# Two layers of mixing and experts: where the modulation blocks, entry loads and sums' zeroing are placed

## The chip, the cores and the metric

One core of one Trainium2 chip. The metric is the time of one execution of the whole kernel on the device, in microseconds (us); less is better. Engines are named as in the profile: PE (TensorE), PEld (its weight loads), DVE (VectorE), ACT (ScalarE), POOL (GpSimd) and SP (the queue that issues most DMAs).

## The reference

Two blocks of different kinds run one after the other on 512 tokens of width 1024, in float32. The change concerns the first, which has two layers and carries 256 context tokens beside the 512.

```python
sc, scc = silu(c), silu(c_ctx)[None]
for i in range(2):
    mods  = sc  @ ada_w[i] + ada_b[i]      # 1024 -> 6 x 1024: sh1, sc1, g1, sh2, sc2, g2
    cmods = scc @ ada_w[i] + ada_b[i]
    h  = rms_norm(x, n1) * (1 + sc1) + sh1            # the same for the context
    p  = h @ w_in                                     # 11 pieces: a_b a_c a_h b_v b_g c_q c_k c_v d_q d_k d_v
    y  = [short conv of a, gated conv of 31 taps of b, window attention of c, global attention of d]
    x  = x + g1 * (y @ w_out)
    h2 = rms_norm(x, n2) * (1 + sc2) + sh2
    x  = x + g2 * expert_choice_ffn(h2)               # 16 experts, each takes its top tokens
```

In the expert step each of 16 experts chooses 64 of the 512 tokens (and, in the first layer, 32 of the 256 context tokens) by a softmax over a router, computes silu(h w_gate) * (h w_up) w_down for them and adds the weighted rows back. Only the first layer updates the context. The modulation vectors are made in 12 blocks of 512 columns each per layer: blocks 0 and 1 are sh1, 2 and 3 sc1, 4 and 5 g1, 6 and 7 sh2, 8 and 9 sc2, 10 and 11 g2.

## The kernel before

All of it is one program; the framework gives every engine its own list of instructions, in an order that it lays out from the order of the Python statements, and puts in the waits. An engine runs its list strictly in order. SP's list holds nearly all loads, so a load whose buffer is not free holds back the loads behind it.

**Modulation blocks.** `ada_gen` (L309) does one block per two steps. A block needs four loads of 512 KB (`ada_load`, L191), 16 PE instructions at L318 (four side by side in column groups), a copy on ACT (L323), four transposes (L327) and two small DVE operations (L329, L330) that leave the vectors in `M[l]`. Loads go into tiles of the pool `wp`, which has five buffers of 512 KB named `raw`; dense weights and five of the expert weight slots use the same five. `ada_gen` also loads the next block ahead (L320).

**Entry (L236 to L398).** SP issues small row loads (gains, biases, conv weights, gathered in `rows` and transposed to columns in `cols` by `rows_to_cols`, L347) mixed with the loads of x, then the four blocks 0, 2, 1 and 3 of layer 0 into a tile of their own, `ada0`, with the context and the first dense weights between them. The key weights of attention c come in one load. The query weights come in two loads of 64 columns (pieces of 256 bytes) per unit. Five row loads are issued by POOL. Each of the six token tiles is scaled by its root mean square and transposed. When all four blocks are done, `norm1_first` (L386) makes the 8 k-slices of the normed input as a high part `hh0` (ACT) and a low part `hl0` (DVE for x, POOL for the context).

**Dense products.** `dense` (L421) goes through units of 128 output columns. Each unit's weights are loaded (`load`), split in two halves into a high part `wh` (ACT, L442) and a low part `wl` (POOL, L443), and multiplied in three products per k-slice (L473, and L475 for the context). `ahead` sets how far in front of the unit the loads run: with 4, one unit ahead after the first four; with None, three.

**Mixing (`layer`, L602).** 18 units of the input projection (order c_k, c_q, c_q, c_v, b, d, a) run interleaved, step by step by fixed shares (`run_all`, L943 to L947), with the attention (`att_gen`), the 31-tap convolution on DVE (`conv31`) and, in layer 0 only, the modulation blocks 4 to 11 of layer 0 and 0 to 7 of layer 1. Layer 0 passes `ahead=4`, layer 1 None. Before it, xT and xcT are stored to DRAM (L621) so that their place can be used, and POOL loads a table (L638) that the rotary step waits for. The output projection (8 units, L999) follows and fills in the expert weights' first loads.

**Routing and experts (`experts`, L1022).** Expert weights come as units of 512 KB, 24 per expert, through a ring of 18 `rawA`, five `raw` and two `rawB` buffers in layer 0 (20, 5 and 8 in layer 1), one new load for each unit that PE has used (`wload`, L1042). In layer 0, 18 are loaded at the start; the five raw ones follow at L1182, as the raw buffers first serve blocks 8 to 11 of layer 1, which are done in steps inside the routing: after the affinities (L1120) and between top-k rounds (L1150). Normed rows are written to `hd` in DRAM, two sum tensors in DRAM are zeroed (3 MB, L1134 to L1139), DVE finds the top tokens, and POOL gathers the rows (L1209), which PE transposes (L1221). Then per expert: gate units, down units of the expert before, up units. In layer 0 the outputs are added into the sums in DRAM by POOL's queue. Near the end the sums are loaded back (`sums_load`, L1305; two buffers) and added to x and the context in 12 halves (`sums_add`, L1310): the four context halves in the up units of expert 15, the eight of x in its down units.

Of the kernel before, what the change touches and what calls it, by code (L numbers as in the profile page):

```python
# [10 lines left out]
F32 = mybir.dt.float32  # L11
# [123 lines left out]
def main_kernel(ctx, tc, I, out, stop=None, dbg=None, manual=False):  # L135
# [37 lines left out]
    dx = pool(ctx, "dx", space=DRAM).tile([128, 8 * 768], F32)  # L173
# [47 lines left out]
    ada0 = ent.tile([128, 4, 4, 1024], F32)  # L221
# [20 lines left out]
    x_load(1)  # L242
    row_load(G, 0, "qn", I["q_norm_g"], 2, dup=True)
    row_load(G, 0, "kn", I["k_norm_g"], 2, dup=True)
    row_load(G, 0, "cbb", I["conv_b_b"].rearrange("l (h p) -> (l h) p", p=128), 4)
    row_load(G, 0, "lng", I["conv_ln_g"].rearrange("l (h p) -> (l h) p", p=128), 4)
    row_load(G, 0, "lnb", I["conv_ln_b"].rearrange("l (h p) -> (l h) p", p=128), 4)
# [3 lines left out]
    x_load(2)  # L251
    SY.dma_start(sinkb, bass.AP(tensor=I["sink"].tensor, offset=I["sink"].offset, ap=[[0, 128], [1, 8]]))
    row_load(SY, 0, "fg", I["final_g"].rearrange("(k p) -> k p", p=128), 8)
    row_load(SY, 0, "ln1", I["ln1_2"].rearrange("l (k p) -> (l k) p", p=128), 8)
    x_load(3)
# [3 lines left out]
    ada_load(0, 0, ada0[:, 0], hfs=(0, 1))  # L259
    row_load(SY, 3, "cq", I["conv_qkv_2"].rearrange("l t (h p) -> (l t h) p", p=128), 48)  # L260
    row_load(SY, 3, "fc", I["ffn_conv_2"].rearrange("l t (h p) -> (l t h) p", p=128), 66)
    ada_load(0, 0, ada0[:, 0], hfs=(2, 3))
    ada_load(0, 2, ada0[:, 2])
    for t in range(2):
        SY.dma_start(cin[:, t, :], I["ctx"][0, t * 128:(t + 1) * 128, :])
    ada_load(0, 1, ada0[:, 1])
    pre0 = {}
    pre0[0] = raw_tile().rearrange("p (k c) -> p k c", k=8)
    SY.dma_start(pre0[0], I["w_in"][0, :, 1536:1664].rearrange("(k p) c -> p k c", p=128))
    pre0[1] = raw_tile().rearrange("p (k c) -> p k c", k=8)  # L270
    for h in range(2):
        SY.dma_start(pre0[1][:, :, 64 * h:64 * h + 64],
                     I["w_in"][0, :, 1280 + 128 * h:1344 + 128 * h].rearrange("(k p) c -> p k c", p=128))
    ada_load(0, 3, ada0[:, 3])
# [34 lines left out]
    def ada_gen(l, blocks, pl, psp):  # L309
        g, o, n = RO["adab"]  # L310
        for b in blocks:
# [8 lines left out]
            if 3 < b < 11 or (l == 1 and b != 7 and b < 11):  # L320
                ada_load(l, b + 1, hfs=range(4 if l == 1 and b > 7 else 3))
# [10 lines left out]
            yield  # L332

# [7 lines left out]
    if True:  # L341
        with ExitStack() as e0:
# [4 lines left out]
            def rows_to_cols(g, n):  # L347
                p = pse.tile([128, 512], F32, name="rc")
                T.transpose(p[:, :n], rows[0:n, g, :], ident[0:n, 0:n])
                V.tensor_copy(cols[:, g, 0:n], p[:, :n])  # L350

            rows_to_cols(0, 16)
            A.activation(s2[:, :, 0], col("c"), AF.Silu)
            A.activation(s2[:, :, 1], col("cc"), AF.Silu)
            ga = ada_gen(0, (0, 2, 1, 3), sqp, pse)
            ss = ent.tile([128, 6], F32)
            for t in range(6):
# [16 lines left out]
                if t == 1:  # L374
                    rows_to_cols(1, RO["n", 1])
# [4 lines left out]
            for g in (0, 2, 3):  # L380
                rows_to_cols(g, RO["n", g])
            V.tensor_scalar(nsink, sinkb, -1.0, None, op0=OP.mult)

        entry.close()

        def norm1_first(sqp):  # L386
            a1 = sqp.tile([128, 8, 2], F32, name="a1")
            for k in range(8):
# [32 lines left out]
        def dense(units, hh, hl, dw, dps, la=3, pre={}, ahead=None):  # L421
# [5 lines left out]
            def load(i):  # L427
                if i in pre:
                    raw[i] = pre[i]
                elif i < len(units):  # L430
                    raw[i] = raw_tile().rearrange("p (k c) -> p k c", k=8)
                    units[i][0](raw[i])

            def split(i):
                if i < len(units):
                    nk = units[i][4] if len(units[i]) > 3 else 8
                    hi[i] = []
                    for a in range(0, nk, 4):
# [3 lines left out]
                        A.activation(wh[:, :n], raw[i][:, a:a + n], AF.Copy)  # L442
                        G.tensor_tensor(wl[:, :n], raw[i][:, a:a + n], wh[:, :n].bitcast(F32), op=OP.subtract)  # L443
# [41 lines left out]
        def colload(src, c0, n=128):  # L485
            def f(raw):
                SY.dma_start(raw[:, :, 0:n], src[:, c0:c0 + n].rearrange("(k p) c -> p k c", p=128))
            return f

        def colload2(src, ca, cb):  # L490
            def f(raw):
                for h, c in enumerate((ca, cb)):
# [529 lines left out]
        def experts(l, rwpA, lg, rbias, a2, nA, nB):  # L1022
# [37 lines left out]
            if has:  # L1060
                ada_load(1, 8)
# [908 lines left out]
```

## Time and profile before

| | us |
|---|---|
| three runs | 2655.12, 2669.66, 2670.03 |
| median | 2669.66 |
| profiled execution, own time | 2663.15 |
| its span, first to last instruction | 2660.6 |

The span is divided like this (from windows and timelines): entry to 48, first mixing and its output projection to 457, routing to 501, first experts to 1075, second mixing and projection to 1360, second routing and experts to about 1890, then the second block. A busy time is what the profile counts for an engine; matmuls overlap, so PE can be "busy" without being at its peak. In a timeline row, the bracket holds the engine's idle time before the instruction and what ended it.

### The profile page before, as it was taken

How to read it: one execution, taken by the hardware profiler on the slowest of the kernel's cores; microseconds unless marked ns; L12 is line 12 of the kernel's file. 1: busy time of each engine (PE TensorE's matmuls, PEld its weight loads, DVE VectorE, ACT ScalarE, POOL GpSimd, SP SyncE). 2: the span in 40 equal slices, each digit the busy share in tenths (PEclk: the TensorE clock that was granted, in tenths of full speed). 3: DMA queues.
4: the chain of work that ended last, by engine and by line, in shares of the span. 5: the costliest groups of instructions: out<-in, count | busy, mean ns of one | idle time of the engine just before them, and what ended most of it. 6: DMA issues, size and time to landing. Idle time of an engine off the chain costs nothing.

```text
span 2660.6 us, 41308 instructions
## 1 busy us (share of the span) xinstructions
PE 2472.6 (93%) x16415; PEld 1498.3 (56%) x16415; DVE 1091.2 (41%) x2371; ACT 870.0 (33%) x1769; POOL 637.3 (24%) x552
## 2 busy tenths in 40 slices
PE   6999999799999999799979989898899999999998
PEld 3776777344444333677743212132578787888876
DVE  4488853311111114689641201021674555444411
ACT  4534362211111111465532111110552435434322
POOL 3423112011111100633220000000433323444443
PEclk9999999899999999799989999999899999999999
DMA  8455455999999998221279999999321102333321
GB/s 284 136 163 141 148 191 195 320 385 387 387 386 385 388 389 296 61 60 48 84 285 391 394 400 400 399 404 408 108 64 27 38 25 72 95 95 96 98 84 63
DMA packets 324758, 584.08 MB, mean 220 GB/s; under 512 B 36864, under 2 KB 190007, under 8 KB 323927
## 3 DMA queue, kind: packets, MB, share of 16 engines
q1 hardware_dynamic: 311943, 555.16, 57.6%
q0 software_dynamic: 12480, 26.23, 4.1%
q8 instruction: 129, 2.11, 0.3%
q14 instruction: 62, 0.51, 0.1%
q10 hardware_dynamic: 144, 0.08, 0.0%
HBM read 556.74 MB, written 18.87 MB: 216 GB/s over the span
## 4 chain that ended last, share of the span: by engine, by line
PE 65%; DMA 18%; DVE 9%; issue 3%; POOL 2%; ACT 1%; SPq 1%; ACTq 0%; DVEq 0%; POOLq 0%
PE px L473 20%; PE ax L1243 4%; DMA rawA<-in_w_down_dram 4%; PE yx L1243 3%; PE ux L1243 3%; PE g L473 2%; DMA rawA<-in_w_up_dram 2%; PE y L584 2%; PE px L475 2%; DMA rawA<-in_w_gate_dram 2%; PE s L553 2%; PE ux L1237 2%; PE pt L565 2%; PE ac L1248 2%; PE ax L1237 2%
## 5 line engine op out<-in xcount | busy, mean ns | idle before, releaser
L443 POOL TENSOR_TENSOR wl<-raw,wh 128x512 fp32r<-128x512 f32 (+1 forms) x312 | 408.7, 1313 | 968.0 <-ACT wh L442 908.2
L442 ACT ACTIVATE wh<-raw 128x512 fp32r<-128x512 f32 (+1 forms) x312 | 193.7, 625 | 440.5 <-PE px L473 207.7
L473 PE MATMUL px<-hh,wh 128*128 128x512 f32 x768 | 314.2, 410 | 6.4 <-DVE xT L1401 1.8
L473 PE MATMUL px<-hh,wl 128*128 128x512 f32 x768 | 311.8, 406 | 6.5 <-POOL wl L443 6.5
L473 PE MATMUL px<-hl,wh 128*128 128x512 f32 x768 | 313.7, 409 | 4.1 <-DVE hl L1019 1.9
L1225 ACT ACTIVATE xt<-tr,mod,a 128x64 f32<-128x64 f32 x256 | 87.0, 405 | 297.6 <-PE tr L1221 287.3
L473 PEld LDWEIGHTS px<-hh,wh 128*128 128x128 f32 x768 | 147.8, 193 | 40.9 <-issue 6.1
L473 PEld LDWEIGHTS px<-hh,wl 128*128 128x128 f32 x768 | 147.9, 193 | 39.5 <-POOL wl L443 7.2
L473 PEld LDWEIGHTS px<-hl,wh 128*128 128x128 f32 x768 | 148.2, 193 | 37.8 <-issue 3.8
L1369 DVE SCALAR_TENSOR_TENSOR Yx<-yx,gcol,Yx 64x512 fp32r<-64x512 f32 x36 | 27.0, 750 | 266.9 <-ACT Yx L1368 266.9
L1209 POOL DMA_INDIRECT xg<-hd,gidx x32 | 29.7, 928 | 432.2 <-PE tr L1221 399.0
L785 DVE SCALAR_TENSOR_TENSOR yT<-ub,cols,yT 128x512 f32<-128x512 f32 (+1 forms) x180 | 126.3, 717 | 0.6
L1243 PE MATMUL ax<-rawA,xt 128*32 128x512 f32 x856 | 117.2, 596 | 1.9 <-DMA rawA<-in_w_gate_dram 1.9
L1273 ACT ACTIVATE sa<-ax 128x512 f32<-128x512 f32 x32 | 19.1, 597 | 287.8 <-PE ax L1243 182.7
L1300 POOL DMA_INDIRECT sumx<-ys,place x14 | 22.0, 1571 | 376.7 <-ACT ys L1347 376.7
L1243 PE MATMUL ux<-rawA,xt 128*32 128x512 f32 x800 | 106.1, 594 | 0.9 <-DMA rawA<-in_w_up_dram 0.9
L1237 PE MATMUL ux<-rawA,xt 128*64 128x512 f32 x328 | 87.5, 611 | 8.3 <-DMA rawA<-in_w_up_dram 8.2
L1237 PE MATMUL yx<-rawA,hT 128*64 128x512 f32 x316 | 80.7, 610 | 12.6 <-DMA rawA<-in_w_down_dram 11.8
L565 PE MATMUL pt<-tab,P 128*128 128x128 f32 x448 | 83.7, 288 | 7.0 <-DVE PT L571 4.3
L1368 ACT ACTIVATE Yx<-yx,gcol 64x512 fp32r<-64x512 f32 x36 | 24.6, 682 | 191.1 <-PE yx L1237 139.3
L1228 DVE TENSOR_SCALAR xt<-tr,a,mod 128x32 f32<-128x32 f32 x128 | 39.1, 310 | 114.7 <-ACT xt L1225 114.2
L1237 PE MATMUL ax<-rawA,xt 128*64 128x512 f32 x316 | 77.4, 612 | 8.1 <-DMA rawA<-in_w_gate_dram 7.5
(593 smaller groups left out, 4887.5 us busy)
## 6 DMA issues: line engine op xcount, KB each, us to landing
rawA<-in_w_gate_dram SPq DMA_DIRECT2D x186, 512.0 KB
rawA<-in_w_up_dram SPq DMA_DIRECT2D x182, 512.0 KB
rawA<-in_w_down_dram SPq DMA_DIRECT2D x151, 512.0 KB
raw<-in_ada_w_dram SPq DMA_DIRECT2D x80, 512.0 KB
raw<-in_w_down_dram SPq DMA_DIRECT2D x74, 512.0 KB
raw<-in_w_gate_dram SPq DMA_DIRECT2D x62, 512.0 KB
raw<-in_w_in_dram SPq DMA_DIRECT2D x56, 512.0 KB
raw<-in_w_up_dram SPq DMA_DIRECT2D x55, 512.0 KB
```

The costliest lines, as they stand in the source:

```text
L442: A.activation(wh[:, :n], raw[i][:, a:a + n], AF.Copy)
L443: G.tensor_tensor(wl[:, :n], raw[i][:, a:a + n], wh[:, :n].bitcast(F32), op=OP.subtract)
L473: T.matmul(px, lhsT=w[:, k % 4, :], rhs=h[:, k0 + k, 0:512], start=st, stop=sp_)
L475: T.matmul(pc, lhsT=w[:, k % 4, :], rhs=h[:, k0 + k, 512:nt], start=st, stop=sp_)
L553: T.matmul(s[:, :w], lhsT=q, rhs=k, start=(a == 0), stop=(a == len(mm) - 1))
L565: T.transpose(pt[:, (t - a) * 128:(t - a + 1) * 128], P[:, t * 128:(t + 1) * 128], ident)
L584: T.matmul(y[64 * g:64 * g + 64, bi * 128:(bi + 1) * 128], lhsT=vs[g][t], rhs=PTs[i, g][t // 4][:, (t % 4) * 128:(t % 4 + 1) * 128], start ...
L785: V.scalar_tensor_tensor(acc[:, j, o:o + n], src, w, acc[:, j, o:o + n], op0=OP.mult, op1=OP.add)
L1225: A.activation(xt[:, kk, 0:64], p[:, k * NX:k * NX + 64], AF.Identity, bias=M[l][:, 24 + kk, 0:1], scale=a2[:, kk, 0:1])
L1237: T.matmul(px[64 * g:64 * g + 64, :], lhsT=lx(u), rhs=w[:, 512 * hf:512 * hf + 512], start=first, stop=last)
L1243: T.matmul(px[32 * g:32 * g + 32, :], lhsT=lx(u)[:, 32 * (g % 2):32 * (g % 2) + 32], rhs=w[:, 512 * hf:512 * hf + 512], start=first, stop= ...
L1248: T.matmul(pc[32 * g:32 * g + 32, :], lhsT=lc(u), rhs=w[:, 256 * q:256 * q + 256], start=first, stop=last)
```

## The change

- Blocks 8 to 11 of layer 1 leave the routing of layer 0. They become `ga` of layer 1's mixing, two steps in each of two phases and four in the last. `experts` starts with `wload(nA + 5)` in both layers, so the raw slots are filled with expert weights at once.
- Layer 1's dense products run with `ahead=4` like layer 0's. Query weights are loaded in pairs: two loads of 512 rows by 256 columns (1 KB pieces) serve two units; the split takes the columns of each unit out of them.
- At the entry, x, blocks 0 and 2, the context, the key weights and blocks 1 and 3 are loaded in this order, then the query pair, then the other small rows, all by SP. `rows` lies in a raw tile.
- Only blocks 0 and 2 are done before the norm. The norm's first four k-slices follow, then the first half of unit 0, then blocks 1 and 3 and the other four k-slices. The remaining rows are turned into columns after unit 0.
- The sums are zeroed in the first mixing, after unit 0, from a 128x512 tile of zeros.
- The context's sums are added in the up units of expert 14, half of x's in those of expert 15, the rest in its down units; the context's sums are loaded an expert earlier.

```diff
@@ entry
-    rows = ent.tile([128, 4, 128], F32)
+    rows = raw_tile()[:, 0:512].rearrange("p (g c) -> p g c", g=4)
+    for t in range(1, 4):
+        x_load(t)
+    ada_load(0, 0, ada0[0])
+    ada_load(0, 2, ada0[2])
+    for t in range(2):
+        SY.dma_start(cin[:, t, :], I["ctx"][0, t * 128:(t + 1) * 128, :])
+    pre0 = {0: raw_tile().rearrange("p (k c) -> p k c", k=8)}
+    SY.dma_start(pre0[0], I["w_in"][0, :, 1536:1664].rearrange("(k p) c -> p k c", p=128))
+    ada_load(0, 1, ada0[1])
+    ada_load(0, 3, ada0[3])
+    def pair_load(src, c0):
+        ts = [raw_tile(), raw_tile()]
+        for i, t in enumerate(ts):
+            SY.dma_start(t.rearrange("p (k c) -> p k c", k=4),
+                         src[512 * i:512 * i + 512, c0:c0 + 256].rearrange("(k p) c -> p k c", p=128))
+        return ts
+    pre0[1] = pre0[2] = pair_load(I["w_in"][0], 1280)
+    row_load(SY, 0, "qn", I["q_norm_g"], 2, dup=True)
...
@@ ada_gen
-                ada_load(l, b + 1, hfs=range(4 if l == 1 and b > 7 else 3))
+                ada_load(l, b + 1, hfs=range(3))
@@ entry's norm
-            ga = ada_gen(0, (0, 2, 1, 3), sqp, pse)
+            ga = ada_gen(0, (0, 2), sqp, pse)
...
-                    norm1_first(sqp)
+                    a1 = cst.tile([128, 8, 2], F32)
+                    norm1_first(range(4), a1)
+                    gd = dense(units, hh, hl, dw, psp, pre=pre0, ahead=4)
+                    next(gd)
+                    drain(ada_gen(0, (1, 3), sqp, psp))
+                    norm1_first(range(4, 8), a1)
+                    entry.close()
@@ dense, split
+                        if len(units[i]) == 6:
+                            src = raw[i][a // 4].rearrange("p (q j c) -> p q j c", j=2, c=64)[:, :, units[i][5], :]
@@ mixing
-                ga = iter(())
                 if has:
...
+                else:
+                    ga = ada_gen(1, range(8, 12), sqp, psp)
+                if not has:
+                    gd = dense(units, hh, hl, dw, psp, ahead=4)
+                g1 = 8 if has else 2
+                if has:
+                    for _ in range(2):
+                        next(gd)
+                    for g in (0, 2, 3):
+                        rows_to_cols(psp, "misc", g, RO["n", g])
+                    zz = sqp.tile([128, 512], F32, name="sq")
+                    G.memset(zz, 0.0)
+                    for acc_, n in zip(accs, (8, 4)):
+                        SY.dma_start(acc_.rearrange("(p a) c -> p (a c)", p=128).rearrange("p (b c) -> p b c", c=512),
+                                     zz[:, None, :].to_broadcast([128, n, 512]))
@@ experts
-            wload(nA if has else nA + 5)
-            if has:
-                ada_load(1, 8)
+            wload(nA + 5)
...
-                    for _ in steps(ga, 2):
-                        pass
...
-                    if has:
-                        zz = sqp.tile([128, 1024], F32, name="ht", bufs=4)
-                        G.memset(zz, 0.0)
...
-                wload(5 if has else 0)
...
-                        if has and e == 15:
-                            sums_add(u)
+                        if has and e == 15 and u % 2:
+                            sums_add(4 + u // 2)
...
                         if has and e == 15:
-                            run_gu("u", e, [], sums_add)
+                            run_gu("u", e, [], lambda u: sums_add(u // 2))
+                        elif has and e == 14:
+                            run_gu("u", e, mid, lambda u: sums_add(8 + u // 2))
...
-                        if has and e in (13, 14):
-                            for t in ((4, 5), range(4))[e - 13]:
+                        if has and e in (12, 14):
+                            for t in ((4, 5), range(4))[e // 2 - 6]:
```

## Rows read from the trace of the kernel before

**Rows 1.** The page's slices of the span: PE's busy tenths, then the DMA engines'.

```profile
PE   6999999799999999799979989898899999999998
...
DMA  8455455999999998221279999999321102333321
```

**Rows 2.** Timeline of the entry: start, us, engine, line, operation, [idle before <-releaser].

```profile
27.49 1.05 ACT L362 ACTIVATE xcT<-cin 128x1024 f32<-128x1024 f32 x1
...
32.72 1.28 DVE L372 TENSOR_TENSOR cin<-xcT,rb 128x512 f32<-128x512 f32 x2 [0.48 <-PE rb L307]
...
44.26 1.05 PE L318 MATMUL misc<-ada,s 128*32 128x512 f32 x4 [0.96 <-DMA ada<-in_ada_w_dram]
...
48.88 0.68 DVE L398 TENSOR_TENSOR hl<-xin,hh 128x512 fp32r<-128x512 f32 x1
...
59.69 0.68 DVE L398 TENSOR_TENSOR hl<-xin,hh 128x512 fp32r<-128x512 f32 x1
...
60.93 1.47 POOL L443 TENSOR_TENSOR wl<-raw,wh 128x512 fp32r<-128x512 f32 x1
...
62.47 0.68 DVE L398 TENSOR_TENSOR hl<-xin,hh 128x512 fp32r<-128x512 f32 x1
...
70.28 1.27 POOL L678 TENSOR_TENSOR sq<-sq,tabl 128x512 f32<-128x512 f32 x1 [2.10 <-DMA tabl<-in_tab_dram]
```

**Rows 3.** Timeline of the routing and the start of the first experts.

```profile
460.49 1.92 PE L318 MATMUL yx<-raw,s 128*32 128x512 f32 x16
...
462.51 0.60 ACT L323 ACTIVATE sq<-yx 128x512 f32<-128x512 f32 x1 [3.00 <-PE yx L318]
...
463.16 0.66 PE L327 MATMUL yx<-tab,sq 128*128 128x128 f32 x4 [0.74 <-ACT sq L323]
...
483.72 1.00 POOL L1209 DMA_INDIRECT xg<-hd,gidx  x1 [6.66 <-DVE tA L1191]
...
494.88 3.43 PE L318 MATMUL yx<-raw,s 128*32 128x512 f32 x8 [13.95 <-DMA raw<-in_ada_w_dram]
...
500.79 1.07 PE L1243 MATMUL ax<-rawA,xt 128*32 128x512 f32 x8
```

**Rows 4.** Timeline of the first experts, PE and SP's queue.

```profile
514.30 4.56 SPq L1055 DMA_DIRECT2D rawA<-in_w_down_dram  x6
...
524.38 0.88 PE L1221 MATMUL tr<-tab,xg 96*128 96x96 f32 x8
...
526.51 1.04 PE L1243 MATMUL ux<-rawA,xt 128*32 128x512 f32 x8
...
527.80 1.04 PE L1243 MATMUL ux<-rawA,xt 128*32 128x512 f32 x8
...
885.72 0.88 PE L1221 MATMUL tr<-tab,xg 96*128 96x96 f32 x8
...
893.14 1.07 PE L1243 MATMUL ax<-rawA,xt 128*32 128x512 f32 x8 [1.13 <-DMA rawA<-in_w_gate_dram]
```

**Rows 5.** Windows, second mixing: bounds, length, engines' busy time, then clock, DMA share, GB/s.

```profile
1210.00:1220.00 10.00, 8.02 (x50) 5.84 (x50) 10.00 (x19) 4.40 (x11) 5.38 (x5) 0.83 0.32 79
...
1300.00:1310.00 10.00, 7.86 (x54) 5.57 (x52) 8.33 (x19) 8.28 (x20) 2.36 (x1) 0.91 0.00 0
```

**Rows 6.** Windows of the entry.

```profile
0.00:5.00 5.00, 0.33 (x2) 0.25 (x3) 0.63 (x5) 1.69 (x4) 3.91 (x11) 1.00 0.56 156
...
25.00:30.00 5.00, 4.01 (x28) 2.34 (x25) 0.90 (x4) 2.97 (x6) 0.00 (x0) 1.00 1.04 392
```

**Rows 7.** The gathered rows' tile, 440 to 560: its transfers.

```profile
DMA to landing us min/median/max: 6.5/8.4/9.9
```

**Rows 8.** Timeline of the end of the first experts.

```profile
1050.52 0.63 PE L1317 MATMUL tr<-tab,rb 128*128 128x128 f32 x4 [1.63 <-DMA rb<-sumx]
```

**Rows 9.** The modulation matmuls' line, 60 to 400: its instructions.

```profile
L318 PE MATMUL misc<-raw,s x256: 592/592/617, 101.2 to 366.8; 128*32 128x512 f32 x128
```

**Rows 10.** Waits of PE, 1095 to 1310: total us, times, longest.

```profile
PE px L473 <- POOL wl L443: 4.4, 1, 4.4
```

More of the change, by code (lines that the diff above doesn't have):

```diff
@@ L172, in main_kernel @@
     xcT = xp.tile([128, 8, 256], F32)
[L173 removed]
+    dxp = pool(ctx, "dx", space=DRAM)
+    dx = dxp.tile([128, 8 * 768], F32)
+    accs = dxp.tile([1024, 512], F32, name="sumx"), dxp.tile([1024, 256], F32, name="sumc")
     stA = cst.tile([128, 768], F32)
@@ L217, in main_kernel @@
     ent = pool(entry, "ent", side="right")
-    rows = ent.tile([128, 4, 128], F32)
+    rows = raw_tile()[:, 0:512].rearrange("p (g c) -> p g c", g=4)
     xin = xip.tile([128, 4, 1024], F32)
     cin = xip.tile([128, 2, 1024], F32)
-    ada0 = ent.tile([128, 4, 4, 1024], F32)
+    entry2 = ExitStack()
+    ada0 = {b: pl.tile([128, 4, 1024], F32, name=f"ada{b}")
+            for pl, bs in ((ent, (1, 3)), (pool(entry2, "ent2", side="right"), (0, 2))) for b in bs}
     def row_load(eng, g, name, ap, n, dup=False):
@@ L332, in ada_gen, with rows_to_cols @@
             yield
+    def rows_to_cols(psp, name, g, n):
+        p = psp.tile([128, 512], F32, name=name)
+        T.transpose(p[:, :n], rows[0:n, g, :], ident[0:n, 0:n])
+        V.tensor_copy(cols[:, g, 0:n], p[:, :n])
     es_l0 = ExitStack()
@@ L345, in main_kernel @@
             pse = Psum(ep, {"tp": 4, "misc": 2, "rb": 1, "rc": 1})
[L347 to L352, printed above, removed]
+            rows_to_cols(pse, "rc", 0, 16)
             A.activation(s2[:, :, 0], col("c"), AF.Silu)
             A.activation(s2[:, :, 1], col("cc"), AF.Silu)
-            ga = ada_gen(0, (0, 2, 1, 3), sqp, pse)
+            ga = ada_gen(0, (0, 2), sqp, pse)
             ss = ent.tile([128, 6], F32)
@@ L379, in main_kernel, with norm1_first @@
             drain(ga)
[L380 to L388, printed above, removed]
+        entry2.close()
+        def norm1_first(ks, a1):
+            for k in ks:
                 if k % 4 == 0:
@@ L429, in load @@
                     raw[i] = pre[i]
+                elif i < len(units) and len(units[i]) == 6 and units[i][5]:
+                    raw[i] = raw[i - 1]
+                elif i < len(units) and len(units[i]) == 6:
+                    raw[i] = units[i][0]()
                 elif i < len(units):
@@ L615, in layer @@
                 psp = Psum(ps, {"px": 3, "s": 2, "pt": 1, "misc": 1, "y": 1}, {"pc": "px"})
+                c0 = dict(a_b=0, a_c=256, a_h=512, b_v=768, b_g=1024, c_q=1280, c_k=1536, c_v=1664,
+                          d_q=1792, d_k=2048, d_v=2176)
+                evs = []
+                units = []
+                for n in "c_k c_q c_v b_g b_v d_k d_q d_v a_c a_h a_b".split():
+                    for j in range(2 if n[2] == "q" or n[0] in "ab" else 1):
+                        nt, ev = NT if n[2] == "q" or n[0] in "ab" else 768, partial(lambda i, px, pc: evs[i](px, pc), len(units))
+                        if n[2] == "q":
+                            units.append((partial(pair_load, w_in, c0[n]), ev, nt, 0, 8, j))
+                        else:
+                            units.append((colload(w_in, c0[n] + 128 * j), ev, nt))
                 if has:
                     hh, hl = hh0, hl0
-                    norm1_first(sqp)
+                    a1 = cst.tile([128, 8, 2], F32)
[5 more added lines that the diff above has]
+                    entry.close()
                     xip_es.close()
@@ L1089, in experts @@
                     psp = Psum(ps, {"tr": 2}, {"misc": "tr"})
-                    ga = ada_gen(1, range(8, 12), mp, Psum(ps, {"yx": 1}, {"misc": "yx"})) if has else iter(())
                     r = roots(sqp, tok_sums(psp, [stA], NTT), NTT, 1.0 / 1024)
@@ L1149, in experts @@
                             V.match_replace(out=D[:NP], in_to_replace=v8, in_values=D[:NP], imm_value=-1.0)
-                        if i in (2, 4, 6):
-                            for _ in steps(ga, 2):
-                                pass
                     tg = hp.tile([80, 128], F32)
@@ L1266, in run_gu @@
                         if each and u % 2:
-                            each(8 + u // 2)
+                            each(u)
                     acc[w, e] = (px, pc)
```

73 lines of the change are left out of this document (20 added, 53 removed).

## The prediction

> **What bounds the kernel now.** I read the page's slices first. TensorE (PE) is busy 9 tenths or more nearly everywhere, so time is to be won only where it waits, or does work that another stage would hide; slices 1, 8, 17 and 21 stand out with 6 or 7, and from slice 8 to 15 the DMA engines are full as well [rows 1]. Then I took the timelines around those places, and windows of 5 and 10 us.
>
> Entry: PE waits for modulation blocks. The last part of the fourth block is there at 44.26, and only then can the norm begin. DVE sets its pace: the first k is done by 48.88 plus 0.68, the seventh six steps of 1.80 later, the eighth at 63.15 [rows 2]. Unit 0's matmuls follow it.
>
> Routing between the first mixing and the first experts: top-k is done and the gather is issued at 483.72, but PE's next instruction in order is a block matmul of the second layer, which waits 13.95 us for its weights; their loads stand behind the zeroing in SP's queue. PE can transpose the gathered rows only after it, at 498.31, and starts expert 0 at 500.79 [rows 3].
>
> First experts: a weight unit takes PE 1.29 us. One expert's period is (885.72 - 524.38)/11 = 32.85 us, 1.369 a unit. No wait for weights stands out until 893.14, where one of 1.13 us comes [rows 4].
>
> Second mixing: PE is nearly always busy, DVE too in its middle; the DMA engines are not [rows 5].
>
> **The change part by part.**
>
> 1. Entry loads. Before the norm's second half can start, x (2.10 MB), four blocks (8.39), context (1.05) and the first key weights (0.52) must land, 12.06 MB. Today small row loads and 256-byte query pieces lie between them. In the new order they come first. With 156 GB/s for the first 5 us and 392 after [rows 6] they end at 5 + (12.06 - 0.78)/0.392 = 33.8; I add 1.2 us for the issue, 35. The two blocks of the first half and the context end two blocks (5.35 us each) and the key weights (1.3) before that, at 23. From the context's landing to its last scaled tile took 27.49 to 34.00, 6.5 us [rows 2], so the first four k run from about 30 to 37.5. From the last block to the first k took 48.88 - 44.26 = 4.62, so the second half's k come at 39.6 and three steps of 1.80 later at 45.0, done at 45.7. Against 63.15 that is 17 us. Two things take some back. Unit 1's two weight splits on POOL, done today before the norm, fall into its second half: where one did so (60.93, 1.47 us), DVE's step took 62.47 - 59.69 = 2.78 instead of 1.80, so 2 x 0.98 = 2 us [rows 2]. The Trainium skill (SBUF — State Buffer, section on two separate sides) says that DVE and GpSimd share a port pair as a lock held for the whole instruction. By that rule two splits of 1.47 us would cost 2.9 instead, and the sum would be 0.9 higher; the row shows the same direction, with the smaller price. Also, the table load on POOL's queue, for which POOL waited 2.10 us at 70.28 [rows 2], now shares the DMA engines with the stores of x and the zeroing; I add 1 us. POOL is what units 1 to 3 wait for in the first mixing, and it starts as much earlier as the norm does. Entry: -14; bounds -17 and 0 (as if all were lost to POOL's queue and the table load).
>
> 2. Row loads on SP's queue instead of POOL's, three transposes of rows, a memset of half the size and the zeroing (3.1 MB, 8 us at 392 GB/s) in the first mixing. The row loads pass the pair load on SP and stand ahead of the next unit's weights, which are wanted three units later. Only the transposes, their copies and the memset can be felt: +1, bounds 0 and +4. The paired query loads save DMA time where nothing waits for it: 0.
>
> 3. Routing. Today the exponential waits for a table load behind the first block's copy on ACT (462.51, after 1.92 us of block matmuls from 460.49), the transposes of the affinities follow a block matmul that waits for its load, and four pairs of small DVE operations lie in the chain [rows 3]. Without them I estimate the gather 4 us earlier, at 479.7. Without zeroing and block loads its rows should land in about 5 us; beside a full queue they needed 6.5 to 9.9 [rows 7]. From transposes to the first expert matmul took 500.79 - 498.31 = 2.5. That gives 487.2 to 487.5 instead of 500.79: -13.3. Lower bound: issue at 483.72, landing after 8.4, matmul at 494.6, -6; upper -15.
>
> 4. The remaining blocks inside expert 0. From 500.79 to 524.38 PE did 12 units [rows 3, 4], 12 x 1.29 = 15.5 us, in 23.6: -8.1. What is late next is the weight stream. It now has all 25 buffers full at the start. The unit waited for at 893.14 is the 281st (12 + 11 x 24 + 4 before it); the 27th was issued at 514.30, so about the 26th landed at 517 [rows 4]. That is (893.1 - 517)/255 = 1.48 us a unit against PE's 1.369; from 25 ahead PE catches up near unit 290, as today near 281. No more is lost than today, as the stream starts earlier by as much as PE. Bounds -8.1 and +2.5 (the last 95 units at the stream's pace, 0.11 each).
>
> 5. Sums spread over three phases instead of two. The same 12 transposed halves; only the wait for a buffer's load, 1.63 us at 1050.52 [rows 8], goes for sure: -1.6, bounds 0 and -4.
>
> 6. Second mixing: four blocks. Per block 16 matmuls in 1.92 and four transposes in 0.66 on PE, a copy of 0.60 on ACT [rows 3], two small DVE operations. PE in full: 4 x 2.58 = 10.3. In the first mixing 16 such blocks run between 101 and 367 [rows 9], among 18 units, and it is the same five buffers; so I take the loads as hidden. PE has gaps of 2 us in windows such as 1210 to 1220 and 1300 to 1310, and DVE is full in the first of them [rows 5]: I take 8. Bounds 0 (all in gaps) and 14 (PE, ACT and DVE in series). The loader now runs one unit ahead instead of three; a unit's load is still issued a unit's time early: 0.
>
> Sum: -14 + 1 - 13.3 - 8.1 - 1.6 + 8 = -28. The profiled execution took 2663.15 (span 2660.6 and 2.55 around it), which gives 2635.2. It lies 6.5 under the median of 2669.66, which gives 2641.7; the three runs straddle it, and I take the middle, 2638.
>
> **The rivals.**
>
> A, the weight stream takes back what PE gains in the first experts. For: the DMA engines show 9 in all those slices [rows 1], and the wait at 893.14. Against: the stream starts earlier too, and with three more buffers full. Price: 95 units by 0.11, 10.6: 2649.
>
> B, the entry's gain is lost: POOL's chain in the first mixing, or the table load behind 6 MB of stores and zeros. For: the 2.10 us wait and the splits' effect on DVE. Against: all of POOL's work moves with the norm. It leaves -4: 2648.
>
> C, the gather itself sets the start: the rows land at 492 whatever PE does. For: it is issued late and shares engines with weights. Against: the prefetch would be over by then. The routing gives 6 instead of 13.3: 2645.
>
> D, the second mixing hides most of the blocks (2 instead of 8), the entry gives its 17, and routing and tail come near their bounds (3 more). For: the gaps [rows 5]. Against: PE shows 9 in all slices of that stage but the first and the last [rows 1]. 2638 - 6 - 3 - 3 = 2626.
>
> E, slower than before. Raw buffers are five; a block takes four. With the loader one unit ahead, each dense unit's weights in the second mixing could wait in SP's queue behind block loads that wait for buffers. One late split cost PE 4.4 us there [rows 10]; for the 14 units after the first four it is 61.6, more than the gain of 36 that stands without the blocks: 2638 - 8 + 61.6 = 2692. It decides from 2.6 us for each of the 14. Against: in the first mixing four times as many blocks go through the same five buffers and PE went through them at an even pace [rows 9].
>
> That the change does not do what it says: the instruction order on each engine could be laid out so that expert 0 starts no earlier. That is C with more lost; it has no case of its own.
>
> **How the numbers follow.** Forecast 0.50 (own range 2626 to 2650), A 0.16, B 0.10, C 0.07, D 0.12, E 0.05. The range reaches from 2615, beyond D, to 2660, where A and B come together. A difference of 1% is 26.7 us here, about what a measurement of this kernel can tell from no change; it lies at 2643, close above the forecast. Faster by more: nearly two thirds of the forecast's case, all of D, a little of the others, 0.54. Slower by over 1%: E and some bad luck, 0.06. Between: 0.40.
>
> **What would show it.** Right: the last context norm operation near 46 instead of 63; expert 0's first matmul some 13 us nearer to the end of the output projection, and its first 12 units in about 16 us; no PE wait for block weights in the routing; the second mixing longer by 5 to 11 us. Wrong: units 1 to 3 waiting longer for POOL, many weight waits before unit 280, a gather that lands over 8 us after issue, or PE waits for weights in the second mixing.

## The result and the profile after

The changed kernel takes 2697.9 us (median of four runs, 2696.43 to 2700.65) against 2664.7 for the kernel before beside it: ratio 1.0133, interval 1.0116 to 1.0150. It is slower by 1.3%; 2638.0 was forecast, and the range ended at 2660. The profiled execution has a span of 2694.7.

Five points found in both traces cut the span: the last `wl` split of the first mixing's projection (POOL), the first expert matmul (PE), the first split of the second mixing, the last split of its projection, the end. The stretches between them, for the two kernels and for the experiments that follow (us, profiled executions):

| kernel | entry, first mixing | routing | first experts | second mixing | rest | span |
|---|---|---|---|---|---|---|
| before | 442.4 | 58.4 | 578.5 | 272.4 | 1308.9 | 2660.6 |
| changed | 437.1 | 45.5 | 622.7 | 279.0 | 1310.5 | 2694.7 |
| 1 no early block | 435.0 | 44.3 | 565.3 | 280.1 | 1311.4 | 2636.0 |
| 2 ring of 22 | 434.3 | 44.0 | 574.3 | 280.4 | 1310.0 | 2643.0 |
| 3 zeroing moved | 430.8 | 44.1 | 567.2 | 279.0 | 1310.8 | 2631.8 |
| 4 blocks alone | 442.7 | 46.6 | 619.6 | 279.0 | 1313.6 | 2701.4 |
| 5 one quarter held | 435.5 | 44.3 | 580.8 | 282.6 | 1311.3 | 2654.4 |
| 6 entry alone | 426.5 | 60.7 | 575.6 | 271.9 | 1310.4 | 2645.0 |
| 7 old sums | 433.2 | 44.2 | 567.0 | 282.9 | 1309.2 | 2636.5 |
| 8 block 8 in routing | 432.2 | 47.6 | 563.1 | 280.1 | 1310.1 | 2633.0 |
| 9 zeroing last | 431.6 | 44.3 | 563.1 | 280.3 | 1308.8 | 2628.1 |
| 10 zeros in raw | 433.8 | 45.5 | 565.3 | 280.1 | 1310.7 | 2635.4 |

The changed kernel gains 5.3 before the routing and 12.9 in it, pays 6.6 in the second mixing, and loses 44.2 in the first experts, where a gain was forecast. The page's slices of the changed kernel already point there (PE's busy tenths, the DMA engines', GB/s):

```profile
PE   7899999899999898798989988899899999999997
...
DMA  8655454799999998233279999999421102333322
GB/s 296 171 164 160 147 201 181 271 350 347 366 363 356 345 360 310 55 118 91 64 303 335 395 394 405 395 404 409 150 71 32 40 18 70 94 94 100 92 86 67
```

Slices 8 to 14 (from 0) still show DMA 9, as in [rows 1], but 345 to 366 GB/s, where the page of the kernel before has 385 to 389 and the second experts' slices 22 to 27 here have 394 to 409. PE, at 9 in slices 8 to 15 before, now has an 8 in 13 and 15. The waits of PE from 484 to 1106 of the changed kernel (total us, times, longest) say for what:

```profile
PE ux L1254 <- DMA raw<-in_w_up_dram: 12.9, 7, 3.6
PE yx L1254 <- DMA raw<-in_w_down_dram: 10.5, 12, 2.3
PE ax L1254 <- DMA raw<-in_w_gate_dram: 9.5, 4, 3.6
PE ax L1254 <- DMA rawA<-in_w_gate_dram: 3.6, 4, 2.0
```

These are 36.5 us of waits for weights, 32.9 of them on the five `raw` slots; [rows 4] had one of 1.13 us, and from 505 to 1079 of the kernel before there are 2.8 us in all. The timeline of SP's queue and PE at the start of the changed kernel's experts (start, us, engine, line, operation) shows the first of them:

```profile
429.93 8.76 SPq L1083 DMA_DIRECT2D raw<-in_w_gate_dram  x2
...
484.96 8.07 SPq L1083 DMA_DIRECT2D rawA<-in_w_down_dram  x7
...
505.00 1.04 PE L1254 MATMUL ax<-rawA,xt 128*32 128x512 f32 x8
...
505.25 1.62 SPq L1083 DMA_DIRECT2D rawA<-in_w_gate_dram  x2
...
508.87 1.04 PE L1254 MATMUL ax<-raw,xt 128*32 128x512 f32 x8
...
509.12 1.81 SPq L1083 DMA_DIRECT2D raw<-in_w_gate_dram  x2
...
516.61 1.94 PE L1254 MATMUL ax<-raw,xt 128*32 128x512 f32 x8 [3.62 <-DMA raw<-in_w_gate_dram]
```

Units 19 to 23 belong in raw buffers. Only two of the five loads go out ahead of the routing (429.93). The third and fourth follow from 509.12 on, as PE gets done with the first two raw units (507.58 and 508.87), behind nineteen loads of later units (two of rawB and the seventeen rawA loads from 484.96 on). So two raw buffers serve five slots. The other three are held, and SP's block loads in the second mixing of the changed kernel show by what:

```profile
1147.89 9.17 SPq L199 DMA_DIRECT2D raw<-in_ada_w_dram  x4
...
1195.56 5.31 SPq L199 DMA_DIRECT2D raw<-in_ada_w_dram  x4
...
1246.06 13.21 SPq L199 DMA_DIRECT2D raw<-in_ada_w_dram  x4
...
1272.57 0.37 SPq L199 DMA_DIRECT2D raw<-in_ada_w_dram  x1
```

Four blocks need 16 loads; here are 13. The other three went out in the first mixing. `ada_gen` loads three quarters of the next block ahead if `3 < b < 11 or (l == 1 and b != 7 and b < 11)`. The second half excludes block 7 of the second layer; the first half asks for no layer, and is true for it. In the kernel before this did no harm, as block 8 was used in the routing. Now it is used at 1154, and three of five raw buffers lie full through the first experts. That is theory H. Its rivals: the loads are laid out badly because 23 of them now stand ahead of the routing (S); only the three missing units of lead count (H2).

### The profile page after: what moved, and what is told of

The parts are those of the page before. It is cut to its first block, busy times and chain, and to the rows that moved or that the text cites. A ratio compares the mean times of both kernels' runs of the same rounds, so it can differ in the third digit from the quotient of the medians.

```text
span 2694.7 us, 41094 instructions
## 1 busy us (share of the span) xinstructions
PE 2483.3 (92%) x16415; PEld 1514.0 (56%) x16415; DVE 1094.8 (41%) x2371; ACT 869.9 (32%) x1769; POOL 632.7 (23%) x545
## 3 DMA queue, kind: packets, MB, share of 16 engines
q1 hardware_dynamic: 300335, 555.16, 57.4%
## 4 chain that ended last, share of the span: by engine, by line
PE 68%; DMA 18%; DVE 8%; POOL 2%; issue 2%; ACT 1%; SPq 0%; ACTq 0%; DVEq 0%; POOLq 0%
PE px L486 20%; PE ax L1254 4%; PE yx L1254 4%; PE ux L1254 3%; DMA rawA<-in_w_down_dram 3%; PE y L591 3%; PE g L486 2%; PE s L560 2%; DMA rawA<-in_w_gate_dram 2%; PE px L488 2%; DMA raw<-in_w_down_dram 2%; PE ac L1259 2%; DMA rawA<-in_w_up_dram 2%; PE yc L1259 2%; PE pt L572 2%; PE ux L1248 2%
## 5 line engine op out<-in xcount | busy, mean ns | idle before, releaser
L1254 PE MATMUL ux<-rawA,xt 128*32 128x512 f32 x800 | 124.3, 593 | 0.0
L1292 DVE TENSOR_TENSOR sa<-ux,sa 128x512 f32<-128x512 f32 x32 | 22.1, 692 | 180.3 <-PE ux L1254 76.6
L1248 PE MATMUL yx<-rawA,hT 128*64 128x512 f32 x316 | 81.5, 621 | 12.9 <-DMA rawA<-in_w_down_dram 12.0
```

The costliest lines, as they stand in the source:

```text
L1248: T.matmul(px[64 * g:64 * g + 64, :], lhsT=lx(u), rhs=w[:, 512 * hf:512 * hf + 512], start=first, stop=last)
L1254: T.matmul(px[32 * g:32 * g + 32, :], lhsT=lx(u)[:, 32 * (g % 2):32 * (g % 2) + 32], rhs=w[:, 512 * hf:512 * hf + 512], start=first, stop= ...
```

## The experiments

**1. No early block.** The changed kernel with

```diff
-            if 3 < b < 11 or (l == 1 and b != 7 and b < 11):
+            if b < 11 and (l, b) != (1, 7) and (l == 1 or b > 3):
```

> Changed kernel, with one condition of ada_gen altered: block 7 of the second layer no longer loads three quarters of block 8 ahead of time, in the first mixing. Theory H (held buffers): in the changed kernel those three raw tiles stay occupied until the second mixing, so the first experts have two raw buffers where their ring counts five; PE's 36 us of waits on weights there (12.9 up, 10.5 down, 9.5 + 3.6 gate) should fall below 5, one expert's period from about 36.5 back to about 33 us, and the time from 2698 to 2650 to 2662. Theory S (the weight loads are laid out badly because the 23 first loads now stand ahead of the routing): the order stays mixed, the waits stay above 30 us, and the time stays within 5 us of 2698.

Measured: 2638.4 us, ratio to before 0.9906 (0.9882 to 0.9929). All five raw loads now go out ahead of the routing, and the loads run in ring order. Their row in SP's queue:

```profile
406.29 30.32 SPq L1083 DMA_DIRECT2D raw<-in_w_gate_dram  x5
```

The waits of PE from 484 to 1045 begin with

```profile
PE ax L1254 <- DMA rawA<-in_w_gate_dram: 3.1, 3, 2.4
```

and hold no other wait for weights. S falls, as all 23 loads stand ahead of the routing here too. H had the cause and missed the size: the first experts are 57.4 us shorter, not 36.5. PE's waits are only the part of the loss that has a name; it also went through its work more slowly. Windows from 520 to 900 (PE's busy time and instructions first; at the end clock, DMA share, GB/s), of the changed kernel and of this one:

```profile
520.00:900.00 380.00, 361.28 (x4173) 154.84 (x4169) 52.41 (x139) 48.12 (x121) 44.84 (x33) 0.99 0.99 354
```

```profile
520.00:900.00 380.00, 380.00 (x4606) 157.14 (x4602) 58.46 (x154) 51.52 (x130) 49.48 (x38) 1.00 1.04 385
```

PE does 10% more instructions in the same 380 us, 5% of them by being busy throughout; what the other 5% is was not itemised. The granted clock, 0.99 in the mean and 0.85 from 880 to 900, is a small part of it. The order in which PE's instructions are laid out had changed as well: gate, down and up units alternate around the late raw units.

**2. A ring of 22.** The three quarters stay where they are, and the ring counts only the buffers that are there.

```diff
-            slots = ["A"] * nA + ["W"] * 5 + ["B"] * nB
+            slots = ["A"] * nA + ["W"] * (2 if has else 5) + ["B"] * nB
...
-            wload(nA + 5)
+            wload(nA + (2 if has else 5))
```

> Changed kernel with the three quarters of block 8 still loaded early, but the ring of expert weights in the first layer made honest: two raw slots instead of five, 22 units in all. Theory H, in its form that the harm is the ring counting on buffers that are not there (SP's queue then stops at a raw load while free rawA buffers stand behind it): waits on weights fall below 10 us, the loads run in ring order, and the time falls to 2652 to 2668, a little above the run without the early block, as the stream is three units nearer. Theory H2 (it is simply three buffers fewer that PE runs into): waits stay above 25 us and the time above 2685. Theory S: within 5 us of 2698.

Measured: 2647.7, ratio 0.9954 (0.9937 to 0.9970): better than H expected, so that form of it holds and H2 falls. In the profiled executions three buffers fewer cost 574.3 - 565.3 = 9 us in the first experts (9.2 by the medians of the whole); the other 48 of the 57 come from a ring that counts on buffers it doesn't have. The longest waits of SP's queue from 520 to 900 for PE show how, first of the changed kernel, then of this one:

```profile
SPq L1083 <- PE yc L1259: 69.8, 45, 5.7
SPq L1083 <- PE ac L1259: 55.2, 18, 8.7
...
SPq L1083 <- PE uc L1259: 18.0, 20, 1.8
```

```profile
SPq L1083 <- PE uc L1259: 19.9, 32, 1.8
SPq L1083 <- PE yc L1259: 14.3, 29, 0.9
SPq L1083 <- PE ac L1259: 12.9, 25, 1.8
```

By these three rows SP waits for PE to release a buffer 143 us in the changed kernel and 47 here, and up to 8.7 us at a time against 1.8. One such stop in the changed kernel, SP's queue and then PE:

```profile
618.31 0.43 SPq L1083 DMA_DIRECT2D rawA<-in_w_gate_dram  x1
626.99 0.33 SPq L1083 DMA_DIRECT2D raw<-in_w_gate_dram  x1
...
628.66 1.54 SPq L1083 DMA_DIRECT2D rawA<-in_w_gate_dram  x2
```

```profile
624.14 1.07 PE L1254 MATMUL ax<-rawA,xt 128*32 128x512 f32 x8
...
625.46 1.04 PE L1254 MATMUL ax<-raw,xt 128*32 128x512 f32 x8
```

From 618.07 to 625.2 PE uses five rawA units, the last at 624.14, and SP issues nothing behind its load of 618.31. It goes on when the first raw unit (625.46) is used. So while SP waits at a raw load, rawA buffers that have come free get no load, as theirs stand behind it. How the 48 us divide between these stops and the changed order of the units on PE was not tried.

**3. Zeroing moved.** Number 1, with the zeroing put before the last phase of the first mixing.

```diff
+                if has:
+                    zz = sqp.tile([128, 512], F32, name="sq")
+                    G.memset(zz, 0.0)
...
                 run_all((gd, 18), (at, w3), (ga, 16 if has else 4), (cv, (42 if has else 21) - c1))
```

> As the run without the early block, and the two sums are zeroed (3 MB of stores) before the last phase of the first mixing instead of right after unit 0. Theory Z: what the entry gained and lost again (units 1 to 2 were 10 and 13 us earlier than before, units 3 and later only 2 to 6) was lost to the stores standing on the DMA engines ahead of POOL's small query transfers (DVE waited 6.8 us for one at 80.09, PE 2.15 us at 83.14); with them gone, the fourth unit's split (89.04 in the changed kernel) comes 6 to 9 us earlier and the time is 5 to 9 us under the run without the early block. Theory P: POOL's and ACT's own chain sets the pace of units 1 to 3 whatever the stores do; the split moves by less than 3 us and the time stays within 3 us of that run.

Measured: 2633.1, ratio 0.9893 (0.9877 to 0.9910). The times of numbers 1 and 3 overlap; the traces differ plainly at the first split of unit 4 (units counted from 0), first number 1, then this one:

```profile
90.34 3.77 POOL L456 TENSOR_TENSOR wl<-raw,wh 128x512 fp32r<-128x512 f32 x3
```

```profile
73.78 1.37 POOL L456 TENSOR_TENSOR wl<-raw,wh 128x512 fp32r<-128x512 f32 x1
```

It comes 16.6 us earlier, and 15.3 earlier than the 89.04 of the changed kernel, more than the 6 to 9 expected, but only 4.2 are left at the projection's last split (430.76 against 434.96). In number 1 DVE waits, between 55 and 110,

```profile
DVE sq L686 <- DMA qC<-sq: 6.8, 1, 6.8
DVE sq L686 <- DMA sumx<-sq: 5.6, 1, 5.6
```

for the query transfer and for the stores of zeros; neither is among its longest waits here. POOL's 128 KB query transfers land 4.5 us after issue (median, 60 to 100) there and 2.4 here.

**4. Blocks alone.** The kernel before, with blocks 8 to 11 done in the second mixing, whose dense loads run one unit ahead as in the changed kernel; the loads ahead of the routing stay 18.

```diff
                     ga = ada_rest()
+                else:
+                    ga = ada_gen(1, range(8, 12), sqp, psp)
...
-            if has:
-                ada_load(1, 8)
```

> The kernel before with one part of the change alone: blocks 8 to 11 of the second layer go from the routing to the second mixing, whose dense loads then run one unit ahead; entry, zeroing, sums and the places of the expert loads are those of before (18 loads ahead of the routing, five raw ones after it). The early load of three quarters of block 8 stays. Theory H: the first experts find two raw buffers, PE waits 30 us or more on weights there, and the time is 2695 to 2715 against 2665. Theory S (it takes the 23 loads ahead of the routing): waits below 5 us and a time of 2648 to 2662, from the routing's 12 and expert 0's 8 less the second mixing's 7.

Measured: 2704.1, ratio 1.0162 (1.0145 to 1.0180). Among PE's waits from 490 to 1108 are again

```profile
PE ux L1236 <- DMA raw<-in_w_up_dram: 14.8, 6, 4.2
PE yx L1236 <- DMA raw<-in_w_down_dram: 8.7, 11, 2.3
PE ax L1236 <- DMA raw<-in_w_gate_dram: 8.5, 4, 2.9
```

So the loss needs neither the entry nor the 23 loads. Moving the blocks past the experts, with the early load as it was, is enough. It gains 11.8 in the routing even here.

**5. One quarter held.** The changed kernel, with one quarter of block 8 loaded early instead of three.

```diff
-                ada_load(l, b + 1, hfs=range(3))
+                ada_load(l, b + 1, hfs=range(1 if (l, b) == (1, 7) else 3))
```

> Changed kernel with one quarter of block 8 loaded early instead of three: four raw buffers for a ring that counts five. By the three runs so far three held buffers cost 59 us (2697.9 against 2638.4), of which three units less of lead are only 9 (2647.7 with the ring made 22). Theory H (the first raw load of a pass that finds no buffer stops SP's queue until PE has used a raw unit of the same pass, so the stream's lead falls from 25 units to as many as there are raw buffers): with four buffers the stop is shorter but there, some 10 to 35 us in all: 2648 to 2675, SP's waits on PE in the first experts between the 41 us of the run with none held and the 143 of the changed kernel. Theory N (only the number of missing units of lead counts): a third of 9, 3 us: 2639 to 2644.

Measured: 2656.5 (2649.55 to 2663.78), ratio 0.9980 (0.9964 to 0.9996). None, one and three held buffers give 2638.4, 2656.5 and 2697.9: 18 us for the first buffer and 21 for each of the next two. SP waits for PE 122 us from 520 to 900 (sum over all its waits for PE), against 54 in number 1 and 144 in the changed kernel; the 41 in the expectation counts only the two longest of number 1's sums (22.5 and 18.4). H holds, and N falls.

**6. Entry alone.** The kernel before with the entry's loads, two blocks before the norm and paired queries; the rest as before.

```diff
-    rows = ent.tile([128, 4, 128], F32)
+    rows = raw_tile()[:, 0:512].rearrange("p (g c) -> p g c", g=4)
...
-            ga = ada_gen(0, (0, 2, 1, 3), sqp, pse)
+            ga = ada_gen(0, (0, 2), sqp, pse)
```

> The kernel before with the change's entry alone (order of the loads, two blocks before the norm and two in it, row loads on SP, paired query loads); sums zeroed, blocks 8 to 11 done, and sums added where before did it. The prediction gave the entry 14 and took 1 back for rows and zeroing. Theory Z (zeroing right behind unit 0 took back 4 to 5 of it): the last split of the first mixing's weights, 442.36 before and 430.76 with the zeroing moved, comes at 429 to 433, and the time is 2649 to 2654 against 2662. Theory R (a part is lost elsewhere, in the attention's chain on DVE and ACT): the split comes at 434 to 438 and the time is 2654 to 2660.

Measured: 2649.5, ratio 0.9961 (0.9947 to 0.9975). The projection's last split comes at

```profile
426.51 1.29 POOL L456 TENSOR_TENSOR wl<-raw,wh 128x512 fp32r<-128x512 f32 x1 [3.00 <-ACT wh L455]
```

15.9 earlier than before (442.4) and earlier than theory Z said; the time is Z's. Number 9 tests its reason.

**7. Old sums.** Number 3, with the sums loaded and added as in the kernel before.

```diff
-                        if has and e == 15 and u % 2:
-                            sums_add(4 + u // 2)
+                        if has and e == 15:
+                            sums_add(u)
```

> As the run with the zeroing moved, but the sums are loaded back and added where the kernel before did it (experts 13 and 14, up and down units of expert 15). The prediction gave the spreading 1.6 (bounds 0 and 4). The traces suggest more: from the gather transposes of expert 13's rows to the second mixing took 193.6 us before (885.72 to 1079.30) and 186.1 in the run without the early block. Theory T1 (the sums make the 7.5): the time rises by 5 to 8, to 2638 to 2641. Theory T2 (only the wait of 1.63 at 1050.52 goes; the rest is the weight stream standing nearer to PE before): it rises by 0 to 3, to 2633 to 2636.

Measured: 2635.5 against 2633.1 (ratios to before 0.9902 and 0.9893, intervals overlapping): T2. From the gather transposes of the thirteenth expert's rows to the second mixing it takes 189.2 us (855.13 to 1044.34) against 187.8 in number 3 (854.24 to 1042.05). The first experts as a whole are equal (567.0 and 567.2), so a price of the sums is not shown.

**8. Block 8 in the routing.** Number 3, with block 8 done in the routing after the rows are written.

```diff
+                    drain(ga)
+                    wload(5 if has else 0)
                     wload(nB - (6 if l else 0))
```

> As the run with the zeroing moved, but block 8 of the second layer, loaded ahead in the first mixing as in the kernel before, is done in the routing while DVE finds the top tokens, and the five raw weight loads follow it; blocks 9 to 11 stay in the second mixing. PE has two idle stretches in the routing (6 us before the transposes of the top tokens, 7.6 for the gathered rows). If a block fits into them for nothing, and it costs a quarter of the second mixing's 7 us: 2631 to 2632. If it delays the chain of the routing (its copy on ACT and its two operations on DVE stand in it) or the raw loads then come late: 2634 to 2642.

Measured: 2634.4 (2631.47 to 2643.28): no different from number 3, and not the gain of the first case. The routing is 3.5 longer, so the block does not fit into it for nothing. The experts are 4 shorter, but no shorter than in number 9, which has no block in the routing; the second mixing, with three blocks, is no shorter than with four.

**9. Zeroing last.** Number 1, with the zeroing behind the last phase of the first mixing.

```diff
                 run_all((gd, 18), (at, w3), (ga, 16 if has else 4), (cv, (42 if has else 21) - c1))
+                if has:
+                    zz = sqp.tile([128, 512], F32, name="sq")
+                    G.memset(zz, 0.0)
```

> As the run without the early block, and the sums are zeroed behind the last phase of the first mixing, ahead of the output projection's later loads, where POOL has no small transfers under way. Theory Z (the zeroing costs what it takes from the small transfers and from the buffer of zeros wherever the attention still runs: 8.5 us right behind unit 0, 434.96 against 426.51 in the entry alone for the last split, and 4.3 before the last phase, 430.76): the last split comes at 426 to 428, and the time is 2627 to 2631. Theory R (what differs from the entry alone lies elsewhere, or the zeroing now delays the weights of the projection or the first experts' loads): the last split at 430 or later and 2632 or more.

Measured: 2632.0, ratio 0.9891 (0.9865 to 0.9916), level with number 3, and the last split at 431.6: not the 426 to 428 of Z. So of the 8.5 us between numbers 1 and 6, some 3 to 4 go with the place of the zeroing, and some 5 come with no stores there at all. Part of these was lost before 105: the same `wl` split stands at 105.08 here and at 101.67 in number 6, 3.4 apart. Windows of 60 to 100 and of 185 to 270, of this kernel and of number 6:

```profile
60.00:100.00 40.00, 34.44 (x178) 27.71 (x177) 17.07 (x35) 15.66 (x32) 27.74 (x27) 0.87 0.51 132
185.00:270.00 85.00, 77.78 (x506) 58.59 (x505) 76.81 (x189) 40.56 (x99) 26.66 (x26) 0.94 0.55 155
```

```profile
60.00:100.00 40.00, 35.12 (x201) 28.06 (x199) 19.12 (x46) 18.58 (x39) 27.77 (x27) 0.96 0.62 164
185.00:270.00 85.00, 78.22 (x549) 57.43 (x549) 79.96 (x197) 42.55 (x102) 24.73 (x22) 1.00 0.53 145
```

In both stretches PE is about as busy in both kernels and does fewer instructions here, at a lower granted clock: 0.09 of 40 us is 3.6, and 0.06 of 85 us is 5. The lag grows to some 7.4 us by the split at 283.24 (275.83 in number 6) and is 5.1 at the last. Number 3 has 0.96 in the first stretch, as number 6, and 0.94 in the second. In number 3 the clock is 0.69 in the 10 us in which PE stood 3.35 us waiting for DVE (at 224.25); number 6 has a wait of 2.35 there and keeps 1.00. In this kernel the lowest stretch is another, 190 to 200 at 0.66, behind 10 us in which PE was busy for 7.26.

The lower clock of the first stretch is not the zeroing's alone: number 1, with the stores right there, has 0.87 from 60 to 100, and so has this kernel, without them. The times of one kernel also go with the clock: the four runs of number 1 took 2629.4 at a mean of 0.976 and 2637.8 to 2641.0 at 0.970 to 0.973. With one trace of each kernel, how much of the 8.5 us belongs to the change and how much to the execution stays open.

**10. Zeros in a raw tile.** Number 1, with

```diff
-                    zz = sqp.tile([128, 512], F32, name="sq")
+                    zz = raw_tile()[:, 0:512]
```

> As the run without the early block, with the sums zeroed right behind unit 0 as there, but the tile of zeros is taken from the five raw buffers instead of the ring of five sq tiles that the rotary step writes. In the run without the early block DVE waits between 55 and 110 us 5.6 for the sq tile that the stores of zeros read and 6.8 for one that a query transfer reads. If the two are separate, the 5.6 goes, the 6.8 stays, and the last split comes 2 to 5 us earlier than 434.96, the time 2633 to 2637. If both come from the DMA engines being full with stores, DVE waits as long in all, and the time stays at 2637 to 2641.

Measured: 2637.7, last split at 433.8. DVE's waits for `sumx<-sq` and the 6.8 for the query transfer are both gone, and two others, 5.9 for the table (2.2 in numbers 1 and 9) and 6.8 for ACT's query copy (5.6 in number 9), stand in their place. The edit also moved the stores: without the wait for an sq tile they are issued at 53.75 instead of 62.80. They now stand beside the table load, issued at 55.47, and the 128 KB query transfers land in 2.4 us again. So the two causes can't be told apart this way; that both come from the stores on the DMA engines fits better, but isn't shown.

## Why the prediction was wrong

The failing step is item 4, in the sentence "It now has all 25 buffers full at the start", with what followed from it, "No more is lost than today, as the stream starts earlier by as much as PE". The stream had 22 buffers and a ring that counted 25. The section on the kernel before says that `ada_gen` loads the next block ahead; I moved the block in the sum without asking which of its loads stay behind and what they occupy until it is done. It could have been counted: the four blocks need 16 loads, and the routing of the kernel before issues 13. Of the signs named beforehand, "many weight waits before unit 280" is one that came. The cost is 57.4 us in the first experts, a term the sum didn't have; without it the median is 2638.4. That this agrees with 2638.0 is partly chance, as the other terms missed in both directions:

- **Entry, rows, zeroing, -13.** Measured -5.3 in the changed kernel, -15.9 for the entry alone. The loads are no longer what the norm waits for, but it doesn't follow them at once. In the changed kernel's timeline the last block's first half on PE waits for DVE (36.31), its second half stands behind the first half of unit 0 (41.76), and only then comes the norm's second half:

```profile
36.31 1.07 PE L326 MATMUL misc<-ada,s 128*32 128x512 f32 x8 [1.29 <-DVE mod L337]
...
41.76 1.07 PE L326 MATMUL misc<-ada,s 128*32 128x512 f32 x8
...
47.52 0.68 DVE L402 TENSOR_TENSOR hl<-xin,hh 128x512 fp32r<-128x512 f32 x1
...
52.96 0.68 DVE L402 TENSOR_TENSOR hl<-xin,hh 128x512 fp32r<-128x512 f32 x1
```

  The norm ends at 53.6, not 45.7; its steps take 1.81, as in [rows 2], and no POOL split of weights fell into them, so the 2 us for that (which counts two splits, though one of unit 1's two lay in the norm before as well, the 60.93 of [rows 2]), and the Trainium skill's larger price for it (SBUF — State Buffer, section on two separate sides), weren't put to the test. The zeroing was "+1, bounds 0 and +4": right behind unit 0 the last split comes 3 to 4 later than with the zeroing elsewhere. The rest goes with stretches at a lower clock, which number 9 has without the stores; one trace each doesn't part the two.
- **Routing, -13.3.** Measured -12.9. The gather is issued 39.4 after the last split instead of 41.4 (2 earlier, not 4) and lands in 4.7, not 6.5 to 9.9 as in [rows 7]; the first matmul starts 1.45 later, instead of the 2.5 of [rows 3]:

```profile
476.43 0.98 POOL L1220 DMA_INDIRECT xg<-hd,gidx  x1 [25.30 <-DVE tA L1202]
...
481.11 1.51 PE L1232 MATMUL tr<-tab,xg 96*128 96x96 f32 x8 [7.54 <-DMA xg<-hd,gidx]
...
482.56 1.90 PE L1254 MATMUL ax<-rawA,xt 128*32 128x512 f32 x8
```

  Rival C was right in that PE now waits for the rows; the wait is part of the 45.5.
- **Blocks inside expert 0, -8.1.** The first 12 units take 16.5 us in the changed kernel (482.56 to 499.01), 17.8 in number 1 (479.28 to 497.12), against the 23.6 of [rows 3, 4]: -7.1 and -5.8. The first matmuls run at the lower clock (below).
- **Weight stream.** Without the held buffers one expert's period is 32.85 us as before, and waits for weights are 3.1 us in all. Rival A has no support here; with 22 buffers it costs 9. The first experts of number 1 are 13.2 shorter than before, where items 4 and 5 gave 9.7; what the rest is was not found, and kernels that are equal in this stage (numbers 1, 3, 9 and 10) differ by 4 (563.1 to 567.2).
- **Sums, -1.6.** 1.4 by the traces of numbers 3 and 7, less than equal kernels differ in this stage: the term is not settled.
- **Second mixing, +8.** Measured +6.6. Number 8 shows that it isn't a price per block; whether the blocks or the loads running one unit ahead make it wasn't tried.

Rival E had the mechanism, loads that stand in SP's queue behind one that waits for a raw buffer, and the right sign. I put it into the second mixing, where there was no such wait, and gave it 0.05.

The fastest kernels are numbers 3 and 9, at 2633.1 and 2632.0, 1.1% under the kernel before; numbers 7 and 8 are not told from them.

## What to carry to other kernels

When a step is moved, follow the loads that are issued for it ahead of time: until the step runs, they hold buffers, and whoever shares the pool in between must count without them. A queue that issues in order turns one buffer that is missing into a stop for all loads behind it, so a ring that counts too many buffers costs far more than a shorter one (57 us against 9 here). PE's waits show where such a loss is and not its whole size; compare the lengths of the stage.

## What the hardware showed unasked

After PE has stood for 7.5 us waiting for the gathered rows, its first eight expert matmuls take 1.90 us instead of 1.04 (482.56 against 505.00 in the changed kernel), near the ratio of the clock's two levels, 1.2 and 2.4 GHz, and the granted clock from 480 to 500 is 0.89; in number 1, after 7.98 us, the same form takes 1.94 twice before it falls to 1.03. So here a wait of 7.5 to 8 us cost a microsecond or two beyond itself. And with 3 MB of stores issued at 62.80, the 128 KB transfers of another queue from 60 to 100 landed in 4.5 us (median, number 1) against 2.4 (number 3); with the stores issued 9 us earlier (number 10) it was 2.4 again.
